# Moving early work and adding unread products between the output projection and the first expert of a hybrid encoder layer

## The chip, the core and the metric

The kernel runs on one core of a Trainium2 chip. The metric is the device time of one execution in microseconds (us). The kernel before takes 1717.46 us, the median of three runs (1713.82 to 1717.86).

## What is computed

One encoder layer over 1024 tokens of width 1024, in float32. Three mixers (retention, a state-space scan and windowed attention) read one input projection, and their outputs go through one output projection and a layer norm. Then a router scores each token for 16 experts, each expert takes the 128 tokens with the highest scores, and a last layer norm follows. Cut to the part around the change:

```python
mix = concat(y_ret, y_ssm, y_att) @ w_out
h = layer_norm(ALPHA * h + mix)                      # 1024 x 1024
aff = softmax(h @ router_w)                          # 1024 x 16
gates, idx = top_k(aff.T, 128)                       # 128 tokens for each expert
xs = h[idx]                                          # 16 x 128 x 1024
hdn = silu(xs @ w_gate) * (xs @ w_up)                # 16 x 128 x 2048
out = (hdn @ w_down) * gates
ffn = zeros.at[idx].add(out)
result = layer_norm(ALPHA * h + ffn)
```

## The kernel before, in words

Tokens lie in eight tiles of 128 rows; the last is `LT` = 7. Products run in a split form: a float32 operand becomes a rounded "high" part and the remainder, its "low" part, and three products (high x high, high x low, low x high) go into the same PSUM bank. `split` (L65 to L75) makes both parts: ScalarE copies the high part, VectorE subtracts for the low part. Line numbers L70, L71 (split) and L79 to L81 (the three products) are those of helpers and so carry many tiles.

The experts' weights come as units of 1 MB, 384 of them and in a fixed order: for each quarter `q` of an expert two units of the gate matrix, two of the up matrix, and two of the down matrix that belong to the quarter before. Unit `k` goes through three steps: `load(k)` (L1286, a DMA issued by SyncE), `high(k)` (L1291, the copy on ScalarE, line L1296) and `low(k)` (L1298, the subtraction on VectorE, line L1303). Five raw buffers hold units before their split: two of a pool `raw`, which units 0 to 3 share, and three of a pool `raw2`, opened only after the router's memory is closed. Six buffers hold split units. `low(k)` frees a raw buffer and issues a later load. One unit feeds one piece of 12 products (L1256).

`last_tile` (L1400 to L1443) is an order written out by hand: in this region each engine takes its instructions in the order of the program (SyncE, which issues the DMAs, too), although a few instructions of the part before, which a planner orders, still run among them (the `rank_after` comparisons, L1035). It does the last two token tiles. For tile 6: transposes of the row block into `rt` (`router_turn`, L878), the router's small products (`router_part`, L892), the softmax (`affinities`, L900), the stores (`out_proj_store`, L927) and the ranks for expert 0 (`rank_tile`, L1039). For tile 7 the output projection is run in parts of the contraction between those steps (`out_proj_part`, L830: the column halves 0 and 1, chunks c0 to c1). Of the first seven tiles the 128 best candidates of expert 0 are ranked and fetched (`candidates_ranked`, `candidates_fetched`, L1052 to L1084; the rows come by an indirect DMA into `xc`). Then `first_slots` (L1087) merges tile 7's scores with the candidates', and `first_turned` (L1103, L1110) makes the transposed token rows of expert 0 by 32 products of 128 columns with two 0/1 matrices (`hits`). `tokens` (L1311) splits them into `xT`. `first_numbers` (L1114) gets their indices and gates. The list for the other experts is sorted in pieces (`top_k`, L1133, a generator) between the products of expert 0.

Two facts of the memory matter. `out_proj_store` scales the tile into `ah` and stores it to `acc_dram`. `ah` shares the one buffer of the tag `rt` with the transposed rows:

```python
K.rt = K.op.tile([P, KC, P], F32, name="rt")        # router_turn, q == 0
ah = K.op.tile([P, D], F32, name="ah", tag="rt")    # out_proj_store
```

And `xT` is a tile of the pool `ex`, which is opened where the router's pools (`tk`, `op`) have been closed.

`quarter(q)` (L1364) runs the pieces. After each piece come a step of the sort, `high` up to four units ahead and `low` three ahead (the lead grows later). A quarter's hidden values (`hid`, L1333 and L1339) are transposed before the next quarter's first piece (L1241).

Of the kernel before, what the change touches and what calls it, by code (L numbers as in the profile page):

```python
# [9 lines left out]
F32 = mybir.dt.float32  # L10
# [10 lines left out]
P = 128  # L21
L = 1024
D = 1024
# [903 lines left out]
def out_proj_store(K, t):  # L927

    nc, z = K.nc, K.Y[t][2]
    nc.sync.dma_start(K.h1_dram[t * P:(t + 1) * P, :], z)  # L930
    ah = K.op.tile([P, D], F32, name="ah", tag="rt")
    nc.scalar.activation(ah, z, AF.Copy, scale=ALPHA)
    nc.sync.dma_start(K.acc_dram[t * P:(t + 1) * P, :], ah)

# [152 lines left out]
def first_slots(K):  # L1087

    nc, tk, t = K.nc, K.tk, LT
    row = rank_row(K, K.aff[:, t, 0:1])  # L1090
    G = rank_before(K, K.crow, t, 0, None)
    ps = K.ptp.tile([P, 4, P], F32, name="tp")
    nc.tensor.matmul(ps[:, 0, 0:1], G, K.order01[:, 1, 0:1], start=True, stop=True)
    rank_before(K, row, t, 2, row)
    r = tk.tile([P, 2], F32, name="last")
    K.hits = [tk.tile([P, P], F32, name=f"hit{i}") for i in range(2)]
    nc.vector.tensor_reduce(r[:, 0:1], K.cnt[:, t], AX.X, OP.add)
    nc.vector.tensor_scalar(K.hits[0], K.slots, r[:, 0:1], None, op0=OP.is_equal)
    nc.vector.scalar_tensor_tensor(r[:, 1:2], ps[:, 0, 0:1], -1.0, K.place, op0=OP.mult, op1=OP.add)
    nc.vector.tensor_scalar(K.hits[1], K.slots, r[:, 1:2], None, op0=OP.is_equal)  # L1100
# [22 lines left out]
    return pt  # L1123


def top_k_rows(K):

    pt = K.ptp.tile([P, 4, P], F32, name="tp")
    K.nc.tensor.transpose(pt[:, 0, :], K.aff.rearrange("p t e -> p (t e)"), K.ident)
    return pt  # L1130


def top_k(K, pt):  # L1133

    nc, pool = K.nc, K.sel
    w = [[pool.tile([P, 64], F32, name=f"w{h}{i}") for i in range(2)] for h in range(2)]
    half = [pool.tile([P, 64], F32, name=f"half{h}") for h in range(2)]  # L1140
    for h in range(2):
        nc.vector.tensor_copy(w[h][0], pt[:, 0, h * 64:(h + 1) * 64])
    for i in range(8):
        for h in range(2):
            nc.vector.max(half[h][:, i * 8:i * 8 + 8], w[h][i % 2])
        for h in range(2):
            if i < 7:
                nc.vector.match_replace(w[h][1 - i % 2], half[h][:, i * 8:i * 8 + 8], w[h][i % 2], -1.0)
        if i in (1, 4):
            yield  # L1150
    yield
    both = pool.tile([P, P], F32, name="both")
    nc.vector.tensor_tensor(both[:, 0:64], half[0], half[1][:, ::-1], OP.max)
    nc.vector.tensor_tensor(both[:, 64:P], half[0], half[1][:, ::-1], OP.min)
    top = yield from bitonic(K, pool, both, P, 32, 3)
    for rows in (64, 32):
        o = pool.tile([rows, P], F32, name=f"o{rows}")
        nc.vector.tensor_copy(o, top[rows:2 * rows, ::-1])
        m = pool.tile([rows, P], F32, name=f"m{rows}")
        nc.vector.tensor_tensor(m, top[0:rows], o, OP.max)  # L1160
        yield
        top = yield from bitonic(K, pool, m, rows, 64, 4)
    rev = pool.tile([32, P], F32, name="rev")
    nc.vector.tensor_copy(rev, top[:, ::-1])
    yield
    pt = K.ptp.tile([P, 4, P], F32, name="tp")
    nc.tensor.transpose(pt[:, 0, 0:32], top, K.ident[0:32, 0:32])
    nc.tensor.transpose(pt[:, 1, 0:32], rev, K.ident[0:32, 0:32])
    m = pool.tile([P, 2, E], F32, name="mm")
    nc.vector.tensor_copy(m[:, 0, :], pt[:, 0, 0:E])  # L1170
    nc.vector.tensor_tensor(m[:, 1, :], m[:, 0, :], pt[:, 1, E:2 * E], OP.max)
    yield
    pt = K.ptp.tile([P, 4, P], F32, name="tp")
    nc.tensor.transpose(pt[0:E, 0, :], m[:, 1, :], K.ident)
    tau = pool.tile([E, 1], F32, name="tau")
    nc.vector.tensor_reduce(tau, pt[0:E, 0, :], AX.X, OP.min)
    taus = pool.tile([E, P], F32, name="taus")
    nc.vector.tensor_copy(taus, tau.to_broadcast([E, P]))
    yield
    pt = K.ptp.tile([P, 4, P], F32, name="tp")  # L1180
    nc.tensor.transpose(pt[:, 0, 0:E], taus, K.ident[0:E, 0:E])
    g = pool.tile([P, 2, NT, E], BF16, name="g")
    for i, op in ((0, OP.is_gt), (1, OP.is_equal)):
        nc.vector.tensor_tensor(g[:, i], K.aff, pt[:, 0, None, 0:E].to_broadcast([P, NT, E]), op)
    yield

    pp = K.ptp.tile([P, 4, P], F32, name="tp").rearrange("p a b -> p (a b)")
    before = pp[:, 0:2 * NT * E].rearrange("p (a t e) -> p a t e", a=2, e=E)
    nc.tensor.matmul(pp[:, 0:2 * NT * E], K.order01[:, 0, :], g.rearrange("p a t e -> p (a t e)"),
                     start=True, stop=False)  # L1190
    for s in range(1, NT):
        nc.tensor.matmul(before[:, :, s:, :], K.order01[:, 1, :], g[:, :, 0:NT - s, :],
                         start=False, stop=False)
    for t in range(NT):
        nc.tensor.matmul(before[:, 1, :, :], K.order01[:, 1, :], g[:, 0, t:t + 1, :].to_broadcast([P, NT, E]),
                         start=False, stop=(t == NT - 1))
    w = pool.tile([P, 2, NT, E], F32, name="sl")
    for i in range(2):
        nc.vector.scalar_tensor_tensor(w[:, i], before[:, i], -float(L), g[:, i], op0=OP.add, op1=OP.mult)
    nc.vector.tensor_tensor(K.slot, w[:, 0], w[:, 1], OP.add)  # L1200
# [60 lines left out]
class Experts:  # L1261
# [36 lines left out]
    def low(self, k):  # L1298

        while self.lows <= min(k, len(self.order) - 1):  # L1300
            k1, self.lows = self.lows, self.lows + 1
            u, raw = self.whl[k1], self.raw.pop(k1).rearrange("p a b -> p (a b)")
            self.K.nc.vector.tensor_tensor(u[:, 1, :], raw, u[:, 0, :].bitcast(F32), OP.subtract)  # L1303
            if k1 != 2:
                self.load(k1 + (2 if k1 < 2 else 5))

    def at(self, when, q, s, fn):

# [1 line left out]

    def tokens(self, e, half, pt):  # L1311

        pool, cs = self.K.ex, slice(half * 4, half * 4 + 4)
        if half == 0:
            self.xT[e] = [pool.tile([P, KC, P], F32R, name=f"xT{s}", bufs=2) for s in range(2)]
        split(self.K, self.xT[e][0][:, cs, :], self.xT[e][1][:, cs, :], pt)
# [80 lines left out]
        self.pg.pop(q - 1, None), self.h.pop(q - 2, None), self.hT.pop(q - 2, None)  # L1397


def last_tile(K, I, O, pool, close):  # L1400

    nc, X, t = K.nc, K.X, LT - 1
    for q in range(2):
        router_turn(K, t, q)
    out_proj_gain(K, t)
    out_proj_shift(K, t)
    X.high(0)
    X.low(0)
    out_proj_part(K, LT, 0, 0, 4)
    for q in range(2):  # L1410
        router_part(K, t, q)
    out_proj_store(K, t)
    out_proj_part(K, LT, 0, 4, 7)
    affinities(K, t)
    token_parts(K, t)
    out_proj_part(K, LT, 0, 7, KC)
    G = rank_tile(K, t)
    out_proj_part(K, LT, 1, 0, 4)
    router_turn(K, LT, 0)
    candidates_ranked(K, G)  # L1420
    out_proj_part(K, LT, 1, 4, 6)
    candidates_fetched(K)
    router_part(K, LT, 0)
    X.high(1)
    out_proj_part(K, LT, 1, 6, KC)
    out_proj_stats(K, LT)
    router_turn(K, LT, 1)
    out_proj_gain(K, LT)
    router_part(K, LT, 1)
    X.high(2)  # L1430
    affinities(K, LT)
    token_parts(K, LT)
    close(*K.psums)
    c_py, K.py = pool("py", space=PSUM, bufs=2)
    c_pg, K.pg = pool("pg", space=PSUM, bufs=3)
    c_pt, K.ptp = pool("ptp2", space=PSUM, bufs=3)
    first_slots(K)
    out_proj_store(K, LT)
    halves = [first_turned(K, half) for half in range(2)]
    pt = first_numbers(K)  # L1440
    rows = top_k_rows(K)
    X.low(1)
    return halves, pt, rows, (c_pt, c_pg, c_py)  # L1443


def expert_add(K, e, py):
# [131 lines left out]
def build(tc, nc, I, O):  # L1578
# [129 lines left out]
    X.load(0)  # L1708
    X.load(1)
    K.psums = c_sm, c_po, c_pa, c_pt, c_ps  # L1710
    halves, pt, rows, psums = last_tile(K, I, O, pool, close)
    close(c_tk, c_op, c_ast, c_s5s, c_hy)
    c_hlb, hlb = pool("hlb", bufs=3)
    hl += [hlb] * 3
    c_ex, K.ex = pool("ex")
    c_raw2, K.raw2 = pool("raw2", bufs=3)
    c_sel, K.sel = pool("sel")
    for half in range(2):
        X.tokens(0, half, halves[half])
        if half == 0:  # L1720
            for k in range(4, 8):
                X.load(k)
            X.high(3)
    X.low(2)
    expert_gather(K, 0, pt)
    X.sort = top_k(K, rows)
    raw0 = []

    def sorted_out():
# [6 lines left out]
    last_rows(X, E - 1)  # L1736
    assert not X.before and not X.after and not X.sort
    hold.__exit__(None, None, None)
    close(raw0[0][0], c_raw2, c_ex, c_hlb, c_raw, c_con, c_hla, *psums)


def layout(inputs):
# [57 lines left out]
```

## Time and profile before

| | |
|---|---|
| median of three runs | 1717.46 us |
| the profiled execution's own time | 1713.62 us |
| its span, first to last instruction | 1711.9 us |
| TensorE busy in the span | 1613.7 us (94%) |
| VectorE busy | 1420.3 us (83%) |
| ScalarE busy | 1089.9 us (64%) |
| GpSimd busy | 321.5 us (19%) |
| mean granted clock of TensorE | 0.973 of full speed |

The span is what lies between the first and the last instruction; the profiled execution's own time is 1.72 us longer. The products of the first expert begin at 555.38 us; the last tile's order, written by hand, takes the 40 us before. PE stands for TensorE's products, PEld for its weight loads, DVE for VectorE, ACT for ScalarE, POOL for GpSimd, SP and SPq for SyncE and its queue of DMA issues. The arrow `<-` in brackets names what ended the idle time ahead of an instruction. The granted clock is 1.00 at 2.4 GHz and 0.50 at 1.2 GHz.

### The profile page before, as it was taken

To read this page: it belongs to the slowest core of one execution; us is meant where nothing else is said; L and a number is where in the kernel's file an instruction comes from. 1 tells how busy PE (TensorE), PEld (TensorE's weight loads), DVE (VectorE), ACT (ScalarE), POOL (GpSimd) and SP (SyncE) were. 2 spreads that over 40 slices of the span, in tenths; PEclk is the share of its full clock that TensorE was granted. 3 is DMA by queue.
4 is the path that set the end of the run, shared out by engine and by line. 5 is a ranking of instruction groups with operands and counts; after the bars stand their busy time and mean duration, and the time that the engine had idled before them with its cause. 6 is when DMAs were issued, how large, how long until landed. Compare 5 with 4: busy or idle time off the path is not lost.

```text
span 1711.9 us, 21285 instructions
## 1 busy us (share of the span) xinstructions
PE 1613.7 (94%) x7738; PEld 1308.9 (76%) x7738; DVE 1420.3 (83%) x1672; ACT 1089.9 (64%) x1157; POOL 321.5 (19%) x442
## 2 busy tenths in 40 slices
PE   6898998799997899999999999999999999999996
PEld 4688876588775678888888888888888777777885
DVE  8687971757766998988988889888888999999995
ACT  3332341567663667777777777777777777777773
POOL 6926800201101001101011010010110313131121
PEclk9999799899998899999999999999999999999998
DMA  6353187923224899999999999999999999999993
GB/s 250 117 143 104 41 247 221 304 93 111 68 74 148 303 361 371 391 408 366 383 391 355 384 375 375 390 358 401 367 381 406 381 376 397 385 415 388 407 411 130
DMA packets 111016, 512.56 MB, mean 299 GB/s; under 512 B 12480, under 2 KB 35264, under 8 KB 60224
## 3 DMA queue, kind: packets, MB, share of 16 engines
q1 hardware_dynamic: 100784, 481.32, 73.3%
q0 software_dynamic: 10128, 29.89, 5.6%
q8 instruction: 61, 1.00, 0.2%
q14 instruction: 43, 0.35, 0.1%
HBM read 465.02 MB, written 46.14 MB: 299 GB/s over the span
## 4 chain that ended last, share of the span: by engine, by line
PE 54%; DVE 16%; DMA 12%; issue 8%; ACT 5%; POOL 3%; SPq 1%; POOLq 0%; DVEq 0%; ACTq 0%
PE gu L1256 25%; PE y L1256 13%; DVE whl L1303 6%; DMA wraw<-in_exp_w_down 5%; DMA zz<-acc_d 3%; PE mm L79 3%; PE mm L81 3%; PE mm L80 3%; ACT whl L1296 2%; PE tp L1241 2%; PE tp L795 1%; DMA wraw<-in_exp_w_up 1%; DMA qs<-q_d 1%; PE at L765 1%; PE po L79 1%
## 5 line engine op out<-in xcount | busy, mean ns | idle before, releaser
L1303 DVE TENSOR_TENSOR whl<-wraw,whl 128x2048 fp32r<-128x2048 f32 x384 | 873.4, 2289 | 95.6 <-ACT whl L1296 95.2
L1296 ACT ACTIVATE whl<-wraw 128x2048 fp32r<-128x2048 f32 x384 | 734.7, 1917 | 241.3 <-PE gu L1256 75.1
L1256 PE MATMUL gu<-whl,xT 128*128 128x512 f32 x3072 | 741.3, 398 | 0.1
L1256 PEld LDWEIGHTS gu<-whl,xT 128*128 128x128 f32 x3072 | 571.4, 189 | 125.7 <-issue 0.3
L1256 PE MATMUL y<-whl,hT 128*128 128x512 f32 x1536 | 368.6, 395 | 0.7 <-ACT hT L70 0.7
L1256 PEld LDWEIGHTS y<-whl,hT 128*128 128x128 f32 x1536 | 288.2, 188 | 69.9 <-ACT hT L70 0.9
L1230 POOL DMA_INDIRECT xs<-h_d,index x15 | 41.4, 2758 | 746.0 <-PE y L1256 488.5
L70 ACT ACTIVATE hT<-tp 128x512 fp32r<-128x512 f32 x80 | 46.3, 584 | 37.5 <-PE tp L1241 22.1
L79 PE MATMUL mm<-hT,whl 128*128 128x512 f32 x160 | 63.7, 398 | 3.0 <-DVE qst L74 2.1
L81 PE MATMUL mm<-hT,whl 128*128 128x512 f32 x160 | 63.1, 395 | 0.0
L80 PE MATMUL mm<-hT,whl 128*128 128x512 f32 x160 | 62.8, 392 | 0.0
L71 DVE TENSOR_TENSOR hT<-tp,hT 128x512 fp32r<-128x512 f32 x80 | 54.4, 683 | 9.6 <-ACT hT L70 9.6
L79 PE MATMUL mm<-WO,yh 128*128 128x512 f32 x128 | 52.8, 412 | 0.5 <-ACT yh L70 0.3
L1241 PE MATMUL tp<-ident,hid 128*128 128x128 f32 x256 | 39.4, 277 | 13.7 <-DVE hid L1339 13.7
L80 PE MATMUL mm<-WO,yh 128*128 128x512 f32 x128 | 51.4, 402 | 0.0
L79 PE MATMUL mm<-whl,hT 128*128 128x512 f32 (+1 forms) x128 | 47.5, 372 | 4.1 <-ACT gate L325 1.8
L1241 PEld LDWEIGHTS tp<-ident,hid 128*128 128x128 f32 x256 | 31.4, 142 | 25.2 <-DVE hid L1339 17.8
L81 PE MATMUL mm<-WO,yl 128*128 128x512 f32 x128 | 50.3, 401 | 0.0
L81 PE MATMUL mm<-whl,hT 128*128 128x512 f32 (+1 forms) x128 | 46.5, 364 | 0.0
L80 PE MATMUL mm<-whl,hT 128*128 128x512 f32 (+1 forms) x128 | 46.4, 365 | 0.0
L775 ACT ACTIVATE S<-S,asm 128x384 f32<-128x384 f32 (+1 forms) x64 | 36.9, 579 | 14.2 <-DVE asm L771 14.1
L1339 DVE TENSOR_TENSOR hid<-hid,gu 128x512 f32<-128x512 f32 x64 | 43.6, 682 | 1.7 <-PE gu L1256 1.6
(435 smaller groups left out, 1909.9 us busy)
## 6 DMA issues: line engine op xcount, KB each, us to landing
wraw<-in_exp_w_gate SPq DMA_DIRECT2D x128, 1024.0 KB, 8.0
wraw<-in_exp_w_up SPq DMA_DIRECT2D x128, 1024.0 KB, 8.0
wraw<-in_exp_w_down SPq DMA_DIRECT2D x128, 1024.0 KB, 8.0
wraw<-in_w_in SPq DMA_DIRECT2D x8, 1024.0 KB, 6.2
x<-in_x SPq DMA_DIRECT2D x8, 512.0 KB, 5.2
h_d<-x SPq DMA_DIRECT2D x8, 512.0 KB, 2.8
wraw<-in_w_out SPq DMA_DIRECT2D x4, 1024.0 KB, 8.0
q_d<-qst SPq DMA_DIRECT2D x64, 64.0 KB, 2.1
```

The costliest lines, as they stand in the source:

```text
L70: nc.scalar.activation(hi, src, AF.Copy)
L71: eng.tensor_tensor(lo, src, hi.bitcast(F32), OP.subtract)
L79: nc.tensor.matmul(ps, a[0], b[0], start=start, stop=False)
L80: nc.tensor.matmul(ps, a[0], b[1], start=False, stop=False)
L81: nc.tensor.matmul(ps, a[1], b[0], start=False, stop=stop)
L775: nc.scalar.activation(S[g][:, :W], S[g][:, :W], AF.Exp, bias=nm[:, g:g + 1], accum_out=rs[:, g:g + 1])
L1230: nc.gpsimd.indirect_dma_start(out=xs, out_offset=None, in_=K.h1_dram, in_offset=bass.IndirectOffsetOnAxis(ap=K.index[:, e:e + 1], axis=0))
L1241: K.nc.tensor.transpose(pt[:, c, :], src[:, (c0 + c) * P:(c0 + c + 1) * P], K.ident)
L1256: nc.tensor.matmul(ps, a[s][c], u[:, t, i * w:(i + 1) * w], start=first and id(ps) not in began, stop=last and left[id(ps)] == 0)
L1296: self.K.nc.scalar.activation(u[:, 0, :], self.raw[k1].rearrange("p a b -> p (a b)"), AF.Copy)
L1303: self.K.nc.vector.tensor_tensor(u[:, 1, :], raw, u[:, 0, :].bitcast(F32), OP.subtract)
L1339: at(self.after, q, 3, lambda: nc.vector.tensor_tensor(self.h[q], self.h[q], self.pg[q][1], OP.mult))
```

## The change

- `out_proj_store`: for tiles 6 and 7 `ah` takes one of the three buffers of the tag `z` (the row blocks), not the `rt` buffer.
- `idle(K, n)`: new; n products of 512 columns on output-projection weights into a PSUM bank that nothing reads. There are 3 after the last part of the projection, 4 after the last transposes, 10 after the last router products and 5 in `first_slots`, 22 in all.
- `low(0)` goes from before the first part of tile 7's projection to before its last part, and with it the issue of load 2. `high(1)` goes ahead (right behind tile 6's softmax), `high(2)` goes behind `first_slots`, and `high(3)` behind both halves of `tokens`.
- The turned rows come ahead of tile 7's store in the program. `xT` has a pool of its own, `xt`, ahead of `ex`.
- The transpose for the sort goes from before the first piece into `top_k`, so behind the first piece.
- Load 7 is issued by `low(2)` and no longer in the list of loads 4 to 7.

```diff
@@ out_proj_store
-    ah = K.op.tile([P, D], F32, name="ah", tag="rt")
+    late = t >= NT - 2
+    ah = K.op.tile([P, D], F32, name="ah", tag="z" if late else "rt", bufs=3 if late else 1)
@@ first_slots
     nc.tensor.matmul(ps[:, 0, 0:1], G, K.order01[:, 1, 0:1], start=True, stop=True)
+    idle(K, 5)
     rank_before(K, row, t, 2, row)
@@ top_k (top_k_rows is gone)
-def top_k(K, pt):
+def top_k(K):
     nc, pool = K.nc, K.sel
+    pt = K.ptp.tile([P, 4, P], F32, name="tp")
+    nc.tensor.transpose(pt[:, 0, :], K.aff.rearrange("p t e -> p (t e)"), K.ident)
@@ Experts.low
-            if k1 != 2:
-                self.load(k1 + (2 if k1 < 2 else 5))
+            self.load(k1 + (2 if k1 < 2 else 5))
@@ Experts.tokens
-        pool, cs = self.K.ex, slice(half * 4, half * 4 + 4)
+        pool, cs = self.K.xt, slice(half * 4, half * 4 + 4)
+def idle(K, n):
+    ps = K.pmm.tile([P, 512], F32, name="gu" if K.pmm is K.__dict__.get("pg") else "mm")
+    for i in range(n):
+        K.nc.tensor.matmul(ps, K.WO[0][:, 0, 0:P], K.WO[0][:, 0, 0:512], start=True, stop=True)
@@ last_tile
     X.high(0)
-    X.low(0)
     out_proj_part(K, LT, 0, 0, 4)
...
     token_parts(K, t)
+    X.high(1)
     out_proj_part(K, LT, 0, 7, KC)
...
     router_part(K, LT, 0)
-    X.high(1)
+    X.low(0)
     out_proj_part(K, LT, 1, 6, KC)
+    idle(K, 3)
     out_proj_stats(K, LT)
     router_turn(K, LT, 1)
+    idle(K, 4)
     out_proj_gain(K, LT)
     router_part(K, LT, 1)
-    X.high(2)
+    idle(K, 10)
     affinities(K, LT)
...
+    K.pmm = K.pg
     first_slots(K)
+    X.high(2)
+    halves = [first_turned(K, half) for half in range(2)]
     out_proj_store(K, LT)
-    halves = [first_turned(K, half) for half in range(2)]
     pt = first_numbers(K)
-    rows = top_k_rows(K)
     X.low(1)
@@ build
+    c_xt, K.xt = pool("xt")
     c_ex, K.ex = pool("ex")
...
         if half == 0:
-            for k in range(4, 8):
+            for k in range(4, 7):
                 X.load(k)
-            X.high(3)
+    X.high(3)
     X.low(2)
```

## Rows read from the trace of the kernel before

**Rows 1.** Busy time by stage: stretch, length, PE, PEld, DVE, ACT, POOL, clock, DMA share, GB/s.
```profile
560.00:570.00 10.00, 8.31 (x36) 6.39 (x34) 10.00 (x50) 7.73 (x6) 0.00 (x0) 1.00 0.88 333
...
590.00:600.00 10.00, 8.17 (x32) 6.25 (x32) 9.76 (x16) 5.41 (x4) 0.00 (x0) 0.83 0.82 305
...
700.00:800.00 100.00, 100.00 (x464) 81.04 (x463) 90.81 (x61) 76.49 (x54) 10.58 (x4) 1.00 0.98 387
```

**Rows 2.** Chain of waits, 480 to 562 us: start, length, engine, tile and line.
```profile
480.64 0.23 PE mm L80
...
525.90 8.13 DMA acc_d<-ah
534.13 0.60 ACT rt L887
...
537.54 0.43 PE mm L79
...
547.05 2.30 DVE whl L1303
549.37 4.86 DMA wraw<-in_exp_w_up
554.25 1.91 ACT whl L1296
...
557.36 2.20 DVE whl L1303
```

**Rows 3.** Timeline of PE, 512 to 573 us.
```profile
527.57 0.29 PE L1016 MATMUL tp<-ident,aff 128*128 128x128 f32 x1 [1.70 <-DVE aff L914]
...
534.78 0.32 PE L1016 MATMUL tp<-ident,cand 128*128 128x128 f32 x1 [1.87 <-ACT rt L887]
...
539.60 0.66 PE L885 MATMUL tp<-ident,z 128*128 128x128 f32 x4 [0.78 <-DVE z L841]
541.50 1.07 PE L897 MATMUL sm<-rwg,rt 128*128 128x16 f32 x8 [1.25 <-DVE rt L889]
545.08 0.45 PE L1016 MATMUL tp<-ident,aff 128*128 128x128 f32 x1 [2.50 <-DVE aff L914]
...
546.80 6.62 PE L1110 MATMUL tp<-hit,z 128*128 128x128 f32 x32 [1.24 <-DVE hit L1098]
...
572.42 0.66 PE L1241 MATMUL tp<-ident,hid 128*128 128x128 f32 x4 [4.11 <-DVE hid L1339]
```

**Rows 4.** Timeline of DVE, 512 to 575 us.
```profile
533.47 0.16 DVE L1080 TENSOR_TENSOR cand<-cand 128x1 f32<-128x1 f32 x1
...
561.58 2.28 DVE L1303 TENSOR_TENSOR whl<-wraw,whl 128x2048 fp32r<-128x2048 f32 x1
```

**Rows 5.** Timeline of ACT, 512 to 562 us.
```profile
553.58 0.60 ACT L70 ACTIVATE xT<-tp 128x512 fp32r<-128x512 f32 x1 [6.10 <-PE tp L1122]
```

**Rows 6.** Timeline of SP's queue, 512 to 556 us.
```profile
524.99 0.33 SPq L1289 DMA_DIRECT2D wraw<-in_exp_w_up  x1
...
553.49 0.81 SPq L1289 DMA_DIRECT2D wraw<-in_exp_w_gate  x2
```

**Rows 7.** Transfers of the tile `ah`, 510 to 560 us.
```profile
DMA to landing us min/median/max: 2.6/2.7/8.1
```

**Rows 8.** Busy time and granted clock in stretches of 2 us.
```profile
530.00:532.00 2.00, 2.00 (x17) 1.71 (x16) 0.99 (x5) 0.00 (x0) 0.00 (x0) 1.00 0.96 377
...
536.00:538.00 2.00, 2.00 (x6) 1.61 (x6) 0.00 (x0) 2.00 (x2) 0.00 (x0) 0.50 0.79 254
...
550.00:552.00 2.00, 2.00 (x11) 2.00 (x11) 0.00 (x0) 0.00 (x0) 0.00 (x0) 0.50 0.74 270
```

**Rows 9.** Timeline of PE, 134 to 153 us.
```profile
135.09 1.95 PE L515 MATMUL at<-U,win 128*128 128x128 f32 x16
136.79 0.48 PE L80 MATMUL mm<-hT,whl 128*128 128x512 f32 x1
```

**Rows 10.** Transfers of the raw units, 515 to 620 us.
```profile
DMA to landing us min/median/max: 4.6/5.1/9.1
```

More of the change, by code (lines that the diff above doesn't have):

```diff
@@ L1123, in first_numbers @@
     return pt
-def top_k_rows(K):
+def top_k(K):
+    nc, pool = K.nc, K.sel
     pt = K.ptp.tile([P, 4, P], F32, name="tp")
-    K.nc.tensor.transpose(pt[:, 0, :], K.aff.rearrange("p t e -> p (t e)"), K.ident)
-    return pt
-def top_k(K, pt):
-    nc, pool = K.nc, K.sel
+    nc.tensor.transpose(pt[:, 0, :], K.aff.rearrange("p t e -> p (t e)"), K.ident)
     w = [[pool.tile([P, 64], F32, name=f"w{h}{i}") for i in range(2)] for h in range(2)]
@@ L1436, in last_tile @@
     c_pt, K.ptp = pool("ptp2", space=PSUM, bufs=3)
+    K.pmm = K.pg
     first_slots(K)
+    X.high(2)
+    halves = [first_turned(K, half) for half in range(2)]
     out_proj_store(K, LT)
-    halves = [first_turned(K, half) for half in range(2)]
     pt = first_numbers(K)
-    rows = top_k_rows(K)
     X.low(1)
-    return halves, pt, rows, (c_pt, c_pg, c_py)
+    return halves, pt, (c_pt, c_pg, c_py)
 def expert_add(K, e, py):
@@ L1710, in build @@
     K.psums = c_sm, c_po, c_pa, c_pt, c_ps
-    halves, pt, rows, psums = last_tile(K, I, O, pool, close)
+    halves, pt, psums = last_tile(K, I, O, pool, close)
     close(c_tk, c_op, c_ast, c_s5s, c_hy)
@@ L1720, in build @@
         if half == 0:
-            for k in range(4, 8):
+            for k in range(4, 7):
                 X.load(k)
-            X.high(3)
+    X.high(3)
     X.low(2)
     expert_gather(K, 0, pt)
-    X.sort = top_k(K, rows)
+    X.sort = top_k(K)
     raw0 = []
@@ L1738, in build @@
     hold.__exit__(None, None, None)
-    close(raw0[0][0], c_raw2, c_ex, c_hlb, c_raw, c_con, c_hla, *psums)
+    close(raw0[0][0], c_raw2, c_ex, c_xt, c_hlb, c_raw, c_con, c_hla, *psums)
 def layout(inputs):
```

## The prediction

> **What bounds the kernel now.** I read the busy time by stage first. From about 610 us on TensorE is busy without a gap in the long expert stage (100.00 of 100 us between 700 and 800 us) while VectorE has 90.81 [rows 1]. So a microsecond won ahead of that stage comes off the end, unless something in between eats it. Between the projection and that stage TensorE isn't the bound. From 557.36 us VectorE works without a gap: all 10.00 us of 560 to 570, still 9.76 of 590 to 600 [rows 1], since the sort for the other experts runs there beside the lows of the units. TensorE meets this as a wait of 4.11 us for the hidden values at 572.42 [rows 3]. What counts is therefore the time at which VectorE's unbroken run begins, `low(2)` at 557.36, and whether that run is fed.
>
> The chain of waits says what sets it [rows 2]. The copy into `rt` at 534.13 waited for the transfer of `ah`, 8.13 us, which had the same buffer. Then comes the last part of the projection at 0.43 us for a product of 512 columns, against 0.23 earlier. The granted clock in these stretches fits: 1.00 at 530 to 532 us, which is 2.4 GHz, and 0.50 from 536, which is 1.2 GHz [rows 8]. In the 10 us ahead of the fall TensorE had two idle times, 1.70 and 1.87 us [rows 3]. The turned rows, 32 products, then take 6.62 us at the low clock [rows 3, 8]. Last in the chain, `low(1)` at 547.05 lets load 3 be issued at 549.37, which lands after 4.86 us; `high(3)` (1.91 us) stands on ScalarE ahead of the second half of `xT`, and only after that comes `low(2)`.
>
> **The parts, as shifts against these rows.**
>
> `low(0)` and `ah`. `low(0)` no longer runs on VectorE ahead of tile 6's softmax (some 2.3 us, as every low in rows 2), so the scores come that much sooner and TensorE's gap of 1.70 closes [rows 3]: -1.7. On SP's queue the two stores of tile 6 stood behind load 2, issued at 524.99 [rows 6]; now they go first, and `ah` lands in 2.7 us rather than 8.1 [rows 7]. Nobody waits for it in `rt` any more. Its new buffer is that of tile 5's rows, long read; the fetched candidates move to tile 6's rows, whose store is out some 5 us before the fetch. The candidates' score is there at 533.63 (533.47 + 0.16, rows 4), yet its transpose ran at 534.78, held by the `rt` copy: another -1.1. Together -2.8 where the last projection part begins.
>
> `low(0)` in its new place covers the time from the candidates' end (533.63 - 1.7 = 531.9) to 534.2. The sum of that projection part isn't due on VectorE before 534.8 (538.86, its start before, less 4.0), so it costs nothing, with 0.6 us to spare.
>
> The clock. With both idle times gone I take the clock to stay at 2.4 GHz. The six products of the last part then take 6 x 0.23 and not 6 x 0.43: -1.2, in all -4.0. The 22 products, 0.23 each, lie in gaps in which TensorE waits for VectorE anyway: three (0.69) in 0.78, four (0.92) in 1.25, ten (2.30) in 2.50, five (1.15) in 1.24 [rows 3]. They write banks that nobody waits for: nothing. If the cover were gone, at 0.43 each, they would cost 3.7 us (0.5 + 0.5 + 1.8 + 0.9).
>
> The turned rows. The nearest row of such a float32 product at full clock is the run of 16 at 135.09, with the next product starting at 136.79, so 1.70 us for 16 [rows 9]. By its length of 1.95, 32 take 3.9; by the starts 3.4. I take 3.5, since the products follow each other here as there: -3.1, in all -7.1. The upper bound is 6.62, no gain. In rows 3 and 8 one product takes 6.62 / 32 = 0.207 us at 1.2 GHz, which is 248 clocks for 128 columns, two passes. The Trainium skill, FP8 and Floating Point Precision, section TensorE Precision Notes, says that true FP32 takes four passes through the array. By that rule and its two levels the products would not get under 0.213 us at 2.4 GHz (an estimate from that page), and 3.1 us of the sum would be gone. The rows speak against it.
>
> Splits of `xT`. The first half waited until 553.58 for the last small product of `first_numbers` [rows 5], since `xT` lay in a pool over closed ones; in its own pool it runs beside the second half. The last turned row ends at 553.42 - 7.1 = 546.3. ScalarE and VectorE then need 1.2 us (556.16, the end of `high(3)`, to 557.36, rows 2) and some 0.15 for the hand-over: `low(2)` begins at 547.7, that is -9.7. Of this -2.6 comes from `high(3)` standing behind the splits and not before them.
>
> Feeding it. `low(1)` shifts by the 4.0 to 543.05, ends at 545.35 and lets load 3 go. With the 4.86 and 1.91 of rows 2 `high(3)` ends at 552.1. VectorE reaches `low(3)`, which began 4.22 us after `low(2)` [rows 2, 4], at 551.9. The later counts: 552.1 against 561.58, **-9.5**. Loads 4 to 6 come once the turned rows have been read (before 553.49, rows 6, now about 546.5), 2.5 us apart; they precede their lows. Load 7 is issued at the end of `low(2)` either way, since it needs that buffer: nothing. `high(1)` and `high(2)` lie in ScalarE's idle time, 6 us of it before the first half's split alone [rows 5]. The sort's transpose now runs after the first piece: TensorE begins that piece at 546.5, 12 x 0.23 later it is 549.3, and VectorE wants it at 550.5. Nothing. TensorE's own earlier start is worth nothing by itself: it only lengthens the wait of 4.11, as VectorE hands over `hid` 9.5 us earlier.
>
> **The sum** is -1.7 - 1.1 - 1.2 - 3.1 - 2.6 and +0.2 for load 3: -9.5 us. Against the profiled execution's 1713.62 that makes 1704.1. That execution lies at the lower end of the runs shown; against the median, 3.8 us above it, I predict **1708.0 us**.
>
> **The rivals.**
>
> 1. *The clock falls all the same.* For it speaks that the stretch keeps short products and transposes and small waits. Against it: at 520 to 532 us the same mix ran at 1.00. The sum then loses 1.2 and 3.1, and the products cost 3.7: -1.5 is left, 1716. Chance 0.10. The Trainium skill, TensorE: Matmul & The Clock Gate, part 4, says that transposes don't count as a busy array for the clock; by that rule only the added products and the few others would hold it, and this rival would be likelier. The rows don't decide it.
>
> 2. *The turned rows don't follow the clock* (any reason, a weight load that binds them among these). Then -6.4, 1711. Chance 0.07.
>
> 3. *Load 3 binds.* It now goes out 4.0 us earlier only, with loads 4 to 6 right behind it. The slowest unit of the stretch took 9.1 us, 4.2 more than taken [rows 10]; then -5.3, 1712. Against it: the loads behind it are issued over a microsecond later and queue after it. Chance 0.09.
>
> 4. *Slower: load 2 binds.* It is now issued at the end of `low(0)`, 534.2 and not 524.99 [rows 6], and `high(2)` stands on ScalarE ahead of `ah`, the hit copies and both halves of `xT`, so all of these and load 3 (behind `ah`'s store on SP) wait for it. With 4.9 us it lands at 539.1. From a landing after 542 on each microsecond comes onto the end; from 551.5, or 17 us after the issue, the kernel is slower than before, and at 22 us by 5 us. The slowest unit took 9.1 [rows 10]. Chance 0.04.
>
> 5. *The gain doesn't come* because the planned part ahead is laid out anew, or the earlier start of the experts is lost where their DMA share is 0.98 [rows 1] and the loads take longer. Then -2 to 0, about 1716.5. Against it: TensorE has no wait for loads in that stage. Chance 0.08.
>
> **How the numbers follow.** The forecast (-7 to -13) has 0.62. Its ends: the turned rows at 3.9 and some load time take 2, and short low-clock stretches in the first quarters that no longer come give 3. The runs of before differ by 4 us. The range 1702.5 to 1715.0 leaves out rivals 4 and 5 and most of rival 1 at the top, 0.18 in all, and next to nothing below. About 0.3% (5.2 us) is what a measurement of this kernel can tell from no change. Faster by more than that, under 1712.3: the forecast, rival 2 and half of rival 3, with something off for the spread of the median, 0.74. Rivals 1 and 5 and the rest make 0.22 within it, and rival 4 gives 0.04.
>
> **What would show it.** The wait of `rt` for `acc_d<-ah` is gone from the chain; the clock is 1.00 from 530 to 547 us; the 32 turned products take about 3.5 us; the first piece of the experts begins at about 546.5 and `low(2)` at about 547.7; the wait for `hid` in the second quarter grows to about 5 to 6 us and ends near 563; the slots for the other experts are ready 9.5 us earlier, and TensorE runs without a gap from about 600. I am wrong if the clock still falls between 530 and 547, if the turned products keep 6.6 us, if VectorE idles between `low(2)` and the end of the sort for loads, or if the shift at 563 isn't found again at the end.

## The result, and the profile after

The changed kernel takes 1709.16 us (median of 18 runs, 1703.77 to 1714.74) against 1717.84 for the kernel before (18 runs, 1709.94 to 1726.68). The ratio is 0.994 with a 95% interval of 0.9926 to 0.9954, so the gain is between 8 and 13 us. The medians lie 8.7 us apart; -9.5 was forecast. The profiled execution took 1704.88 us with a span of 1703.2 (before 1713.62 and 1711.9).

The part ahead of the change isn't equally long in every execution: VectorE starts tile 6's gain (L919) at 519.22 us in the trace of before and at 520.37 after, and at up to 526.01 in the runs below. So the two are compared by **the stretch**, from that start to the start of `low(3)`: 42.36 us before (to 561.58, [rows 4]), 32.79 after. That is -9.57. Of the timeline of VectorE before, tile 6's gain and `low(2)`:

```profile
519.22 1.28 DVE L919 SCALAR_TENSOR_TENSOR z<-z,l1mv,g 128x1024 f32<-128x1024 f32 x1
...
557.28 2.28 DVE L1303 TENSOR_TENSOR whl<-wraw,whl 128x2048 fp32r<-128x2048 f32 x1
```

The timeline of VectorE after, 515 to 566 us (the first line is tile 6's gain, then `low(0)`, the last sum, the second 0/1 matrix, `low(1)`, `low(2)` and `low(3)`):

```profile
520.37 1.28 DVE L919 SCALAR_TENSOR_TENSOR z<-z,l1mv,g 128x1024 f32<-128x1024 f32 x1
...
533.04 2.29 DVE L1300 TENSOR_TENSOR whl<-wraw,whl 128x2048 fp32r<-128x2048 f32 x1
535.70 0.69 DVE L841 SCALAR_TENSOR_TENSOR z<-z,mm 128x512 f32<-128x512 f32 x1 [0.36 <-PE mm L81]
...
543.63 0.29 DVE L1102 TENSOR_SCALAR hit<-slots,last 128x128 f32<-128x128 f32 x1
543.84 2.29 DVE L1300 TENSOR_TENSOR whl<-wraw,whl 128x2048 fp32r<-128x2048 f32 x1
...
548.87 2.28 DVE L1300 TENSOR_TENSOR whl<-wraw,whl 128x2048 fp32r<-128x2048 f32 x1
...
553.16 2.28 DVE L1300 TENSOR_TENSOR whl<-wraw,whl 128x2048 fp32r<-128x2048 f32 x1
```

`low(0)` ends at 535.33, before the last sum can start: it lies in idle time. The timeline of TensorE after, the lines that answer to [rows 3] (the lines of L1400 are the added products):

```profile
526.88 0.28 PE L1017 MATMUL tp<-ident,aff 128*128 128x128 f32 x1
...
533.08 0.29 PE L1017 MATMUL tp<-ident,cand 128*128 128x128 f32 x1 [0.86 <-DVE cand L1081]
...
536.44 0.66 PE L885 MATMUL tp<-ident,z 128*128 128x128 f32 x4
536.85 1.18 PE L1400 MATMUL mm<-WO 128*128 128x512 f32 x4
538.31 1.07 PE L897 MATMUL sm<-rwg,rt 128*128 128x16 f32 x8 [0.28 <-DVE rt L889]
539.22 2.58 PE L1400 MATMUL mm<-WO 128*128 128x512 f32 x10
...
543.59 4.00 PE L1112 MATMUL tp<-hit,z 128*128 128x128 f32 x32
...
564.02 1.12 PE L1238 MATMUL tp<-ident,hid 128*128 128x128 f32 x4 [5.03 <-DVE hid L1335]
```

The gap of 1.70 us is gone, of the 1.87 there are 0.86 left, those of 0.78, 2.50 and 1.24 are filled and that of 1.25 but for 0.28, and the turned rows take 4.00 us and not 6.62. The wait for the hidden values is longer, as it should be.

The `x` at the end of a line counts the trace's records, and a plain float32 product has two of them: the 4 router products of `router_part` stand there as x8, and the turned rows are 16 products (two halves, four chunks, two matrices), not 32 as the text ahead says, shown as x32. The added products, in the rounded type, and the transposes have one each (x4, x10). Busy time and clock after, in stretches of 2 us ([rows 8] before):

```profile
536.00:538.00 2.00, 1.92 (x10) 1.06 (x8) 1.88 (x5) 0.00 (x0) 0.63 (x2) 1.00 0.72 197
...
546.00:548.00 2.00, 2.00 (x19) 1.93 (x18) 0.81 (x2) 0.81 (x2) 0.00 (x0) 1.00 0.47 84
...
562.00:564.00 2.00, 0.00 (x0) 0.00 (x0) 2.00 (x3) 2.00 (x2) 0.00 (x0) 0.50 0.98 414
```

The last line lies in the wait for the hidden values, in which the clock falls; no run filled this gap.

The timeline of ScalarE after ([rows 5] before): the halves of `xT` follow the turned rows, and `high(3)` waits behind them for load 3.

```profile
545.84 0.60 ACT L70 ACTIVATE xT<-tp 128x512 fp32r<-128x512 f32 x1 [1.58 <-PE tp L1112]
547.63 0.60 ACT L70 ACTIVATE xT<-tp 128x512 fp32r<-128x512 f32 x1 [1.19 <-PE tp L1124]
551.08 1.92 ACT L1293 ACTIVATE whl<-wraw 128x2048 fp32r<-128x2048 f32 x1 [2.85 <-DMA wraw<-in_exp_w_up]
```

### The profile page after: what moved, and what is told of

It reads as the page before. It is cut to its first block, busy times and chain, and to the rows that moved or that the text cites. A ratio compares the mean times of both kernels' runs of the same rounds, so it can differ in the third digit from the quotient of the medians.

```text
span 1703.2 us, 21330 instructions
## 1 busy us (share of the span) xinstructions
PE 1610.9 (95%) x7760; PEld 1306.0 (77%) x7760; DVE 1421.5 (83%) x1672; ACT 1090.4 (64%) x1157; POOL 329.9 (19%) x442
## 4 chain that ended last, share of the span: by engine, by line
PE 56%; DVE 14%; DMA 12%; issue 7%; ACT 5%; POOL 3%; SPq 2%; POOLq 0%; DVEq 0%; ACTq 0%
PE gu L1253 26%; PE y L1253 13%; DVE whl L1300 5%; DMA zz<-acc_d 4%; DMA wraw<-in_exp_w_down 3%; PE mm L79 3%; PE mm L80 3%; PE mm L81 3%; ACT whl L1293 2%; PE tp L1238 2%; DMA wraw<-in_exp_w_up 1%; PE tp L795 1%; PE sm L897 1%; SPq L723 1%; DMA wraw<-in_w_out 1%
```

## The experiments

Each kernel was profiled once; a single run's time says little here (the changed kernel's own runs lie 11 us apart), so the stretch decides, and times are given for kernels with several runs. The stretch itself repeats well: after, and the runs 3, 9 and 11, whose edits hardly touch it, have 32.79, 32.91, 32.77 and 32.76 us. From `low(3)` to the last instruction the traces of before, after and the runs 1 to 8, 10 and 11 have 1147.8 to 1154.3 us (1150.3 before, 1150.0 after), with no link to the stretch that can be seen. So no trace shows that what is won there is lost later, but a spread of 6.5 us would hide a small loss, and it blurs single times.

| run (products: the added ones) | stretch, us | turned rows, us |
|---|---|---|
| before | 42.36 | 6.62 |
| after | 32.79 | 4.00 |
| 1 without products | 34.28 | 5.50 |
| 2 before, `ah` only | 40.61 | 5.72 |
| 3 `ah` back in `rt` | 32.91 | 4.00 |
| 4 `high(3)` back | 38.54 | 4.00 |
| 5 `low(0)` back | 34.62 | 4.00 |
| 6 `xT` back in `ex` | 34.15 | 4.00 |
| 7 products doubled | 36.09 | 3.73 |
| 8 before, products only | 42.58 | 4.00 |
| 10 before, `high(3)` only | 38.85 | 5.27 |
| 11 transposes for products | 32.76 | 4.00 |

**1. Without the products.** The question that the prediction had settled by assumption.

```diff
 def idle(K, n):
+    return
```

> The changed kernel without its 22 extra products; nothing of the output is left out. The stretch is counted on VectorE from the start of tile 6's gain (L919) to the start of low(3): 42.36 us before (519.22 to 561.58), 32.79 after (520.37 to 553.16). Theory: the clock stays because the two idle times of 1.70 and 1.87 us ahead of its fall are gone, and the products only fill gaps. Then the clock is 1.00 from 530 to 547 us, the 32 turned products keep 4.0 us, the stretch stays at 32.8 and the time within 1 us of the changed kernel (1709). Rival: the products are what holds the clock. Then it falls to 0.50 somewhere between 530 and 547, the turned rows take up to 6.6 us and products of 512 columns 0.43, and the stretch grows by up to 1.2 + 3.1 = 4.3 us, the time to about 1713.

Neither is right as a whole. Busy time and clock of this run:

```profile
540.00:542.00 2.00, 1.07 (x8) 0.97 (x8) 1.87 (x4) 0.00 (x0) 0.20 (x1) 1.00 0.98 406
542.00:544.00 2.00, 0.13 (x1) 0.17 (x1) 1.92 (x5) 1.78 (x3) 0.22 (x1) 0.57 0.43 176
544.00:546.00 2.00, 0.76 (x4) 0.53 (x5) 1.61 (x11) 1.72 (x4) 0.91 (x5) 0.50 0.66 262
...
548.00:550.00 2.00, 2.00 (x15) 2.00 (x15) 0.15 (x2) 0.60 (x1) 0.00 (x0) 0.72 0.27 61
```

The clock stays at 2.4 GHz through the whole projection: that comes from the waits removed. It falls only in the router's tail, where TensorE was busy 1.07 and then 0.13 of 2 us, and comes back within the turned rows, which take 5.50 us. So the products hold the clock over the last 5 us, for 1.5 us of the stretch. The other traces agree. In all nine with the early moves and with work in the gaps (after, runs 3 to 7, 9, 11 and 12) the clock is 1.00 to the end of the turned rows. In the four without such work (before, 1, 2 and 10) it falls ahead of them. The time, 1707.35 us (6 runs), ratio 0.9917 to before with an interval of 0.9894 to 0.9941, can't be told from that of the changed kernel.

**8. The products alone**, in the kernel before.

```diff
     out_proj_part(K, LT, 1, 6, KC)
+    idle(K, 3)
... (and the 4 and the 10)
     nc.tensor.matmul(ps[:, 0, 0:1], G, K.order01[:, 1, 0:1], start=True, stop=True)
+    idle(K, 5)
```

> The kernel before with the 22 products alone, at the same places. Theory: the wait for rt lies ahead of all of them, so the clock falls to 0.50 near 536 us as before; the first seven cost 0.43 us each, 1.0 us more than their gaps; with TensorE busy the clock then comes back and stays, the turned rows take 4.0 us, but that gain is hidden behind load 3 and high(3): stretch 43.4 us, 1.0 over before. Rival: the clock stays low to the end of the turned rows and all products cost: 45.2 us. Rival: products alone bring the gain: under 41 us.

As expected but for the 1.0 us, which didn't come: the turned rows start 27.60 us behind tile 6's gain, 27.58 before. The clock fell, came back while the first products ran, and the turned rows had it whole. What they gain by it, 2.6 us, doesn't show in the stretch, since load 3 and `high(3)` come later than the rows.

```profile
542.00:544.00 2.00, 2.00 (x10) 1.81 (x10) 0.00 (x0) 2.00 (x3) 0.14 (x1) 0.62 0.51 104
544.00:546.00 2.00, 2.00 (x6) 1.52 (x6) 0.31 (x1) 1.87 (x2) 0.00 (x0) 0.53 0.39 158
546.00:548.00 2.00, 2.00 (x11) 1.14 (x9) 1.84 (x5) 0.00 (x0) 0.37 (x1) 1.00 0.00 0
```

**7. Twice the products.**

```diff
-    for i in range(n):
+    for i in range(2 * n):
```

> The changed kernel with 44 extra products, twice as many in each of the four places. Theory: the 22 fill the gaps to the brim (0.69 of 0.78, 0.92 of 1.25, 2.30 of 2.50, 1.15 of 1.24 us), so each further one costs its 0.23 us less what is left of the gap: 0.45 + 0.5 + 2.2 + 1.0, so the turned rows start 4.1 us later and the stretch is about 36.5 us. Rival: there is still room, or TensorE runs ahead: 33 to 34 us.

+3.3 us in the stretch; the turned rows start 26.78 us behind tile 6's gain and not 23.22, which is +3.56 (4.1 expected). The 22 fit because their number fits. The rows themselves take 3.73 us here and not 4.00: both 0/1 matrices were made well before.

```profile
550.61 0.29 DVE L1102 TENSOR_SCALAR hit<-slots,last 128x128 f32<-128x128 f32 x1
```

```profile
551.55 3.73 PE L1112 MATMUL tp<-hit,z 128*128 128x128 f32 x32
555.12 0.17 PE L1123 MATMUL tp<-tok,hitb 128*128 128x5 bf16 x1
```

**11. Transposes in their place.**

```diff
-    for i in range(n):
-        K.nc.tensor.matmul(ps, K.WO[0][:, 0, 0:P], K.WO[0][:, 0, 0:512], start=True, stop=True)
+    for i in range(2 * n):
+        K.nc.tensor.transpose(ps[:, i % 4 * P:(i % 4 + 1) * P], K.hold[:, i % 8 * P:(i % 8 + 1) * P], K.ident)
```

(`K.hold` is a tile that is long there; 44 transposes.)

> The changed kernel with 44 transposes of 128 columns (0.11 us each) in the places of the 22 products of 512 columns (0.23 us each), so the same time on TensorE. Without any, the clock fell at about 543 us and the turned rows took 5.5 us, stretch 34.3. Theory A, by the Trainium skill, TensorE: Matmul & The Clock Gate, part 4, transposes don't count as a busy array: the same fall, 34.3 us. Theory B: what counts is that TensorE has work in its gaps, transposes too: the clock is 1.00 from 530 to 550, the turned rows take 4.0 us, stretch 32.8.

Theory B. The timeline of TensorE in this run; the granted clock is 1.00 in every 2 us from 526 to 552.

```profile
540.16 2.38 PE L1400 MATMUL mm<-ident,b 128*128 128x128 f32 x20
...
544.52 4.00 PE L1112 MATMUL tp<-hit,z 128*128 128x128 f32 x32
```

**2 and 3. The buffer of `ah`**, given to the kernel before (the diff), and taken from the changed one (its reverse).

```diff
-    ah = K.op.tile([P, D], F32, name="ah", tag="rt")
+    late = t >= NT - 2
+    ah = K.op.tile([P, D], F32, name="ah", tag="z" if late else "rt", bufs=3 if late else 1)
```

> The kernel before with one edit: ah of tiles 6 and 7 in the buffers of the rows and not in rt. Theory: the candidates' transpose no longer waits for the rt copy (-1.1) and with only one idle time of 1.70 us left the clock stays at 1.00, so the last six products of the projection win 1.2 us and the turned rows 2.6 to 3.1; but the turned rows' gain is hidden, since low(2) still stands behind load 3, high(3) and the second half of xT, and these only come with low(1): stretch 42.4 - 2.3 = 40.0 us. Rival: the clock falls all the same: stretch 41.2, turned rows 6.6 us. Rival: the buffer is all there was: the stretch goes to 34 or less.

> The changed kernel with ah back in the one buffer of rt. Theory: what held rt was load 2 ahead of the stores of tile 6; now load 2 is issued 10 us after them, ah lands some 2.7 us after its issue at 524.5, before the copy into rt at 530.5. So the stretch stays at 32.8 us, and the own buffer is worth nothing once load 2 has moved. Rival: the shared buffer is what cost the 8 us: the copy into rt waits to 533 or later, the candidates' transpose with it, and the stretch grows by 2 us or more.

Run 2: the candidates' transpose waits for their score alone, and the clock holds to the end of the projection; the last sum comes 2.46 us earlier against the gain of tile 6. Then the clock falls in the router's tail at about 543, the four router products (eight records) take 1.89 us and not 1.07, and of the 2.46 us 1.75 are left. The idle time of 1.70 us was still there in this run, so the wait for `rt` alone had cost the projection its clock.

```profile
538.37 0.29 PE L1017 MATMUL tp<-ident,cand 128*128 128x128 f32 x1 [0.86 <-DVE cand L1081]
...
543.60 1.89 PE L897 MATMUL sm<-rwg,rt 128*128 128x16 f32 x8 [1.21 <-DVE rt L889]
```

Run 3: the stretch is 0.12 us longer, nothing. Either cure removes the wait: another buffer, or load 2 out of the way of the stores. In the changed kernel the buffer is the idle half of the pair. In run 3 the copy into `rt` waits for the transposes and not for a transfer:

```profile
535.54 0.60 ACT L887 ACTIVATE rt<-tp 128x512 f32<-128x512 f32 x1 [2.46 <-PE tp L885]
```

**5. `low(0)` in its old place.**

```diff
     X.high(0)
+    X.low(0)
     out_proj_part(K, LT, 0, 0, 4)
...
-    X.low(0)
     out_proj_part(K, LT, 1, 6, KC)
```

> The changed kernel with low(0), and load 2 behind it, back in the old place ahead of tile 6's router products. Theory: it stands on VectorE ahead of tile 6's softmax again, TensorE's gap of 1.70 us returns, and everything behind moves by it: stretch 32.8 + 1.7 = 34.5 us. The clock stays at 1.00, since the later wait for rt is not there. Rival: the place it left is as dear, as it now stands ahead of the projection's last sum: stretch 32.8, no loss. Rival: with load 2 ahead of the stores again, the candidates' fetch into tile 6's rows waits for the store: stretch 37 or more.

34.62: the theory, to 0.1 us. The gap is back, with 1.68 us, and the clock stays at 1.00.

**4 and 10. `high(3)`**, between the halves in the changed kernel (the diff), and behind them in the kernel before (its reverse).

```diff
-    X.high(3)
+            X.high(3)
```

> The changed kernel with high(3) between the two halves of tokens again, as before the change. Theory: ScalarE then waits for load 3 (it was there at 551.08) ahead of the second half of xT, which comes at 553.0 and not at 547.63, and low(2) starts 5.3 us later: stretch 38.1 us, of the whole gain of 9.6 more than half. Rival, by the sum of the prediction: the order is worth 2.6 us, stretch 35.4. Rival: the second half is hidden behind load 3 anyway, stretch 32.8 to 33.5.

> The kernel before with one edit: high(3) behind both halves of tokens. Theory, the term of 2.6 us in the sum by itself: the second half of xT follows the last turned row at once, low(2) starts 2.6 us earlier and load 3 has landed long before low(3): stretch 39.8 us. Rival: without the other edits nothing is won, since the second half waits for something else too: 42.4. Rival: it wins more than 4 us, as much as its loss in the changed kernel: 37.5 or less.

Run 4 loses 5.75 us. The second half of `xT` stands behind a wait of 5.18 us for load 3 (ScalarE), and VectorE and TensorE behind that:

```profile
554.65 1.91 ACT L1293 ACTIVATE whl<-wraw 128x2048 fp32r<-128x2048 f32 x1 [5.18 <-DMA wraw<-in_exp_w_up]
556.46 0.58 ACT L70 ACTIVATE xT<-tp 128x512 fp32r<-128x512 f32 x1
```

Run 10 wins 3.51 us. Of this 1.86 come from the order (2.00 us from the last turned row to `low(2)`, before 3.86), and 1.64 from turned rows that ended earlier: the clock was up for more of them.

```profile
554.00:556.00 2.00, 2.00 (x19) 2.00 (x18) 0.00 (x0) 0.00 (x0) 0.00 (x0) 0.92 0.50 102
```

The edited order comes behind the rows, so the 1.64 isn't its doing. The same edit is thus worth 1.9 us alone and 5.75 in company, because the other edits bring the turned rows forward by 7 us and load 3 by 4.

**6. `xT` in its old pool.**

```diff
-        pool, cs = self.K.xt, slice(half * 4, half * 4 + 4)
+        pool, cs = self.K.ex, slice(half * 4, half * 4 + 4)
```

> The changed kernel with xT back in the pool ex. Theory: the first half's split waits for the last small product of first_numbers again (about 547.6 us and not 545.84), so both splits stand one behind the other after the turned rows and low(2) starts some 0.7 us later; load 3 binds low(3) no more than it did: stretch 32.8 + 0.7 = 33.5 us. Rival: the pool is what lets the loads or the first piece go early: 35 us or more. Rival: hidden behind load 3: 32.8 to 33.0.

+1.36 us, twice the 0.7 expected. Both splits begin only when the memory of the closed pools is free. `first_numbers` is done with it at 549.43, but what ends the wait is the transfer of tile 7's `ah`, which lay there too. TensorE's first piece then waits 1.45 us for the splits.

```profile
550.22 1.09 ACT L70 ACTIVATE xT<-tp 128x512 fp32r<-128x512 f32 x2 [4.15 <-DMA acc_d<-ah]
```

**9 and 12. Attempts to beat both kernels.** After the change VectorE is the bound from 548.87 us to the end of the sort, while GpSimd has nothing to do. Run 9 gives it three lows.

```diff
-            self.K.nc.vector.tensor_tensor(u[:, 1, :], raw, u[:, 0, :].bitcast(F32), OP.subtract)
+            eng = self.K.nc.gpsimd if k1 in (4, 8, 12) else self.K.nc.vector
+            eng.tensor_tensor(u[:, 1, :], raw, u[:, 0, :].bitcast(F32), OP.subtract)
```

> The changed kernel with the lows of units 4, 8 and 12 on GpSimd in place of VectorE. Theory: from low(2) to the end of the sort VectorE is the bound, so each low taken from it brings the handed-over values forward by up to 2.2 us, as far as TensorE waits: the wait of 5.03 us for the hidden values falls to about 2.8, and the kernel wins 2 to 4 us over the changed kernel. A low of half the size took 3.2 us on GpSimd at the start of the kernel before (L71), so one takes some 6.4 us and low(4) ends near 563, just when TensorE wants unit 4. Rival: VectorE runs slower beside GpSimd, or unit 4 or the load behind it comes late: no gain, or 1 to 4 us lost.

The rival: ratio 1.0001 to the kernel before (0.998 to 1.0022; 12 runs), so the whole gain is lost. GpSimd's timeline in this run:

```profile
569.94 4.67 POOL L1301 TENSOR_TENSOR whl<-wraw,whl 128x2048 fp32r<-128x2048 f32 x1 [6.43 <-ACT whl L1293]
```

VectorE's timeline beside it:

```profile
570.43 4.26 DVE L958 TENSOR_TENSOR b<-b 128x64 f32<-128x64 f32 x1
574.61 0.21 DVE L959 TENSOR_TENSOR b<-b 128x64 f32<-128x64 f32 x1
```

And the wait of TensorE for the sort (in total, times, longest), 1.61 us in the changed kernel:

```profile
PE tp L1164 <- DVE b L959: 8.2, 1, 8.2
```

A two-input VectorE instruction of 0.22 us stood until GpSimd's ended at 574.61. Beside the other two moves a low took 4.49 us (2.28 by itself) and another step of the sort 4.54, and the sort's transpose comes 38.02 us after `low(3)`, 31.66 in the changed kernel. The Trainium skill, SBUF — State Buffer, section Who interferes with whom, says that a VectorE instruction with two SBUF inputs contends with a GpSimd instruction that reads SBUF, for ports that are locked to one of them. The trace agrees, 4.26 us for 0.22.

Run 12 leaves the lows on VectorE and runs them two units ahead of the products, not three, until piece 14.

```diff
-        return 3 + sum(n >= i for i in (16, 30, 44))
+        return 2 + sum(n >= i for i in (14, 16, 30, 44))
...
-            self.high(min(lead + 1, self.taken + self.RING))
+            self.high(min(max(lead + 1, self.taken + 4), self.taken + self.RING))
```

> The changed kernel with the lows two units ahead of the products and not three until piece 14 (the highs stay four ahead), so that one low fewer stands on VectorE ahead of the first hidden values and of the sort's end. Theory: VectorE's unbroken run after low(2) is what TensorE waits for at 564.02 (5.03 us) and at 584.82 (1.61 us); with one low of 2.2 us put off beyond both, both points come some 2 us earlier, and with the low's catching up hidden in the later stage the kernel wins about 2 us over the changed kernel. Rival: the put-off low is late for its own piece, or the loads behind it are: the waits only move to other places, no gain.

The first wait falls from 5.03 to 2.82 us, and the sort's transpose comes 62.30 us after tile 6's gain (64.45 in the changed kernel), though waits for late lows take its place:

```profile
563.67 0.66 PE L1238 MATMUL tp<-ident,hid 128*128 128x128 f32 x4 [2.82 <-DVE hid L1335]
...
583.43 1.19 PE L1253 MATMUL y<-whl,hT 128*128 128x512 f32 x4 [1.16 <-DVE whl L1300]
584.55 0.24 PE L1164 MATMUL tp<-ident,b 32*128 32x32 f32 x1
```

At the fourth quarter's transposes (623.36 us here, 623.71 after) the lead over the changed kernel is still 2.2 us. From there to the end this trace takes 1085.7 us and that of the changed kernel 1079.5, so the lead isn't found again; whether the edit or the spread of that part is the reason stays open. The time is 1709.58 us (6 runs), ratio 0.9931 to before (0.9905 to 0.9956): better than the kernel before, but the runs can't tell it from the changed kernel.

## Why the prediction was right, step by step

The terms measured, in the prediction's order, are -2.85, -1.51, -2.62, -2.58 and nothing for load 3, against -2.8, -1.2, -3.1, -2.6 and +0.2. That the sum came to -9.57 is in part luck: one term was 0.5 us too large, two others were 0.5 short together.

- **Where the time is set** (VectorE's run from `low(2)` on, and after it a stage in which TensorE is the bound): right. `low(2)` moved by -9.56 us (-9.7 forecast) and `low(3)` by -9.57 (-9.5); the wait for `hid` grew to 5.03 us (5 to 6), and it ended 9.55 us earlier against tile 6's gain.
- **`low(0)` and the `rt` wait**, -2.8: measured -2.85 at the candidates' transpose. Run 5 shows the part of `low(0)`. The new buffer of `ah` was not needed for it: run 3.
- **The clock**, -1.2 and the products at nothing: the size about held (the turned rows start 4.36 us earlier, 4.0 forecast), the reason only half. The step that failed is the sentence that with both idle times gone the clock stays. Run 1 shows that it does so through the projection (run 2: the wait for `rt` gone is enough) but not through the router's tail; there the products hold it, and are worth 1.5 us of the stretch. They were costed at no loss, which is right: the turned rows start 23.22 us behind tile 6's gain with them and 23.21 without. But no gain was seen in them.
- **The turned rows**, -3.1: measured -2.62, the term that was mis-sized most. The 3.5 us is counted to the next start but taken from 6.62, a length (6.45 to the next start); that is 0.17. And the second 0/1 matrix is made from 543.63 to 543.92, while the products have begun at 543.59; in run 7, where it is there before them, they take 3.73 us and not 4.00, which is 0.27. Counted to the next start run 7 has 3.57 us, near the 3.5: two alternating matrices cost nothing that shows, and the row chosen was right.
- **"Two passes"** was a misreading that changed no term. The 0.207 us is the time of a record, and a product has two. In run 7 a product takes 3.57 / 16 = 0.22 us at 2.4 GHz, and the 16 records of [rows 9] are 8 products of 1.70 / 8 = 0.21. The Trainium skill, FP8 and Floating Point Precision, section TensorE Precision Notes, says four passes for true FP32, and the prediction's estimate from it is 0.213 us for a product: the trace agrees with that page. Taken for products, the rule would not have cost the sum 3.1 us: 16 x 0.213 is 3.4.
- **Splits and `high(3)`**, -2.6: -2.58 (3.86 us from the last turned row to `low(2)` before, 1.28 after). Run 4 shows what the sum couldn't: the term isn't a constant but grows with how late load 3 is, 5.75 us in company.
- **Load 3**, the later of two: right to 0.2 us, but VectorE's own work was the later: `high(3)` ends at 553.0, and the first step of the sort ends where `low(3)` begins, 553.16, 4.29 us after `low(2)` (before 4.30). Rivals 3 and 4 didn't come: load 2, issued at 535.37 on SP, was there for `high(2)` at 540.53 without a wait.
- **What wasn't in the sum**: from `low(3)` to the experts' slots after the sort (L1205, L1208 before) it takes 45.44 us after and 46.97 before. The clock was low for part of the 6 us behind the sort's transpose before, and wasn't after. No trace ties that to the change: TensorE waits 0.8 to 1.9 us there in the other traces too, except runs 9 and 12; in runs 7, 9 and 10 the clock fell and in most it didn't. I take it for chance. The earlier `high(1)` and `high(2)`, the later store, the sort's transpose and load 7 were not taken out one by one; the terms above leave no room for more than 0.1 us of them in the stretch.

## What to carry to other kernels

Look for the transfer that holds a shared buffer, and at what stands ahead of it on its queue: moving the load behind it was worth as much here as another buffer (runs 2 and 3). Idle time of TensorE was priced twice, by itself and by the clock of what followed; unread work of the length of the gap, products or transposes, kept the clock, but work beyond the gap cost most of its time (run 7: 3.6 us, 4.1 expected). And a step's worth depends on its company: test it by taking it out of the whole, not only by itself.

## What the runs showed that was not expected

Transposes hold the clock as well as products do (run 11: 1.00 throughout, 4.00 us for the turned rows, against 5.50 with nothing in the gaps). The Trainium skill, TensorE: Matmul & The Clock Gate, part 4, says that a transpose doesn't count as a busy TensorE in the same way, and that the full clock doesn't engage for it; here the measurement decides, and rival 1 of the prediction had no support from that rule. And a low on GpSimd took 4.5 to 4.7 us, less than the 6.4 worked out from the smaller one, yet stopped VectorE's two-input instructions to its end.
